# Grouped-query mixer: the value projection issued ahead of the first query projection blocks

## The chip, the cores and the metric

The kernel runs on one core of a Trainium2 chip. The metric is the device time of one execution in microseconds (us); lower is better. Before the change it is 1267.39 us, the median of 3 runs (1267.34 to 1268.09).

## What is computed

A two-layer encoder trunk over 512 tokens of width 1024, in float32. The change lies in the mixer of the second layer, which is grouped-query attention: 16 query heads of 64 share 4 key and value heads.

```python
def odd_mixer(x, mix_norm, w_qkv, q_norm, k_norm, w_out):
    proj = rms_norm(x, mix_norm) @ w_qkv
    q, k, v = jnp.split(proj, [GQA_Q_WIDTH, GQA_Q_WIDTH + GQA_KV_WIDTH], axis=-1)
    q = rms_norm(q.reshape(Bsz, S, GQA_HEADS, GQA_HEAD_DIM), q_norm)
    k = rms_norm(k.reshape(Bsz, S, GQA_KV_HEADS, GQA_HEAD_DIM), k_norm)
    v = v.reshape(Bsz, S, GQA_KV_HEADS, GQA_HEAD_DIM)
    q = apply_rope(q, cos, sin)
    k = apply_rope(k, cos, sin)
    return gqa_block_attention(q, k, v) @ w_out
```

Ahead of it stand the first layer (neighbourhood attention with a state-space scan, then a feed-forward network), behind it a second feed-forward network. Each sub-layer adds its result to `x`.

## The kernel before

Activations lie with the model dimension on the 128 partitions, as 8 tiles of 128 x 512. Every float32 operand is split in a high and a low part (`_h`, `_l`), and a product is three matmuls: high weight by low data, low weight by high data, high by high (`mm3`, lines 162 to 167). A weight block arrives as `_r` by a DMA that SP issues (line 151), ACT rounds it to the high part (line 152), and DVE subtracts to get the low part (line 154). The raw buffer has 2 turns, the high and low ones 3 each.

The mixer's projections are blocks of 24 matmuls of 512 columns (8 tiles of `x` by three): `kpa` and `kpb` for the keys, then for each of 4 head groups g two query blocks `q{g}_0` and `q{g}_1` (`q_blocks`, line 1251). The value projection `gv0` to `gv3` (lines 1375 to 1403) is 4 blocks of 24 matmuls of 256 columns; its weights `wgv` come in two DMAs and are split in four pieces by ACT and DVE, and its result is scaled and split into `gvt0` to `gvt3`. Query and key blocks take turns on 3 PSUM banks, so that a block waits until the block three before it has been read. Score tiles, value blocks and the head norms (`ok_ss`, `oq_ss`, line 1213) share 2 other banks (tag `s`).

When both query blocks of a group are there, `q_finish` (line 1270) makes them ready for the scores: DVE applies the rotary tables (lines 1171 to 1173), PE sums squares over a head (line 1213), DVE and ACT make the reciprocal root (lines 1215, 214 to 216, 208, 209), DVE multiplies (line 1275), ACT and DVE split (lines 1182, 1183; for groups 1 to 3 the split runs on POOL), and SP issues 16 DMAs that stack the parts into `QS{g}_0` to `QS{g}_3` (line 1188). Likewise 16 DMAs stack the keys into `K0` to `K3`.

Attention is a loop of 32 steps i, two per head. A step's `scores` (line 1286) are two tiles `os` of 128 x 512: two matmuls (lines 1293, 1294), a row maximum on DVE (line 1296), an exponential with row sum on ACT (line 1298), a reciprocal on DVE (line 1300), and a scaling on POOL (line 1302). Two steps later `transposes` turns the tiles on PE (line 1311), and ACT and DVE split the turned tile (lines 1314, 1315); three steps later `values` multiplies with `gvt` (lines 1328, 1329) into `oc`.

The source lays the rest of the projections between those steps: a generator `fill` yields after every three matmuls of the query blocks of groups 1, 2, 3 and of the output projection; 8 pieces are drawn ahead of the loop (`OD_FILL`), and then as many per step as `OD_QUOTA` says (5, 5, 4, 2, ...). What is written is a priority and not the final order: for this part of the kernel a list scheduler decides the order on each engine from the dependencies, the buffers and its own estimate of when an operand is ready. The built program's order, shown below, is what each engine follows; it takes its instructions strictly one after another.

Of the kernel before, what the change touches and what calls it, by code (L numbers as in the profile page):

```python
# [77 lines left out]
def encoder_kernel(ctx: ExitStack, tc: tile.TileContext, xt, vec, cst, rope, nab, w_v, w_qk, w_dt, w_ssd,  # L78
                   w_o0, w_t0, w_fa, w_fb, w_kv, w_gv, w_gq, w_o1, out):
    nc = tc.nc  # L80
    V, A, G, T = nc.vector, nc.scalar, nc.gpsimd, nc.tensor
# [13 lines left out]
    def bank(name, tag="p"):  # L95
        if tag in turns:
            turns[tag].append(turns[tag].pop(0))
            tag = turns[tag][-1]
        return pp.tile([P, S], F32, name=name, tag=f"p{tag}", bufs=BANKS[tag])

    def slot(name, dt=F32):
        return sp.tile([P, S], dt, name=name, tag="s")
# [15 lines left out]
    def f(ap):  # L118
        return ap.bitcast(F32)
# [24 lines left out]
    def load_w(src, cols, name, eng=None, los=None):  # L144
        hi = wsp.tile([P, 1024], F32R, name=f"{name}_h", tag="wh", bufs=WH)
        lo = wsp.tile([P, 1024], F32R, name=f"{name}_l", tag="wl", bufs=WL)
        raw = wsp.tile([P, 1024], F32, name=f"{name}_r", tag="wr", bufs=WR)[:, 0:cols]
        parts = src if isinstance(src, list) else [src]
        for n, part in enumerate(parts):
            w = cols // len(parts)  # L150
            nc.sync.dma_start(raw[:, n * w:(n + 1) * w], part)
        A.activation(hi[:, 0:cols], raw, AF.Copy)  # L152
        def low():
            (eng or V).tensor_tensor(lo[:, 0:cols], raw, f(hi)[:, 0:cols], ALU.subtract)  # L154

        if los is None:
            low()
        else:
            los.append(low)
        return hi, lo  # L160

    def mm3(ps, w, wc, x, xc, first, last, wn=P, skip=False):
        (wh, wl), (xh, xl) = w, x
        a, b = slice(wc, wc + wn), xc
        T.matmul(ps, wl[:, a], xh[:, b], start=first, stop=False, skip_group_check=skip)  # L165
        T.matmul(ps, wh[:, a], xl[:, b], start=False, stop=False, skip_group_check=skip)  # L166
        T.matmul(ps, wh[:, a], xh[:, b], start=False, stop=last, skip_group_check=skip)  # L167
# [3 lines left out]
    def stream(blocks, ahead):  # L171
        ws = []
        for n, (_, matmuls) in enumerate(blocks):
            while len(ws) < min(len(blocks), n + 1 + ahead):
                ws.append(blocks[len(ws)][0]())
            yield from matmuls(ws[n])
# [974 lines left out]
    def odd_mixer(op):  # L1151
# [89 lines left out]
        def after(steps, fn):  # L1241
            later.append([steps, fn])

        def step(flush=False):
            for item in list(later):
                item[0] -= 1
                if flush or item[0] <= 0:
                    later.remove(item)
                    item[1]()

        def q_blocks(g, eng):
            banks = []

            def matmuls(w):
                banks.append(bank(f"q{g}_{len(banks)}"))
                for k in range(KB):
                    mm3(banks[-1], w, k * P, xg[k], ALL, k == 0, k == KB - 1)
                    yield
                sq = slot(f"oqsq{g}_{len(banks)}")
                A.activation(sq, banks[-1], AF.Square)  # L1260
                sqs.append(sq)
                if len(sqs) == 2:
                    V.tensor_tensor(sqs[0], sqs[0], sqs[1], ALU.add)
                    after(OD_AFTER, lambda: q_finish(g, banks, sqs[0]))

            sqs = []
            for n in range(2):
                yield (lambda n=n: load_w(w_gq[2 * g + n], 1024, f"wq{g}_{n}", eng)), matmuls

        def q_finish(g, banks, sq):  # L1270
            ra, rb = rotate(*banks, qtab, f"q{g}")
            r = head_rstd(sq, f"oq{g}")
            eng = G if g else V
            for t in (ra, rb):
                V.tensor_tensor(t, t, r, ALU.mult)
            (ah, al), (bh, bl) = split(ra, f"qa{g}", eng=eng), split(rb, f"qb{g}", eng=eng)
            QS = []
            for j in range(4):
                qs = lane(f"QS{g}_{j}", "qs", 7, F32R)
                stack(qs, (ah, bh, al, bl), j)  # L1280
                QS.append(qs)
            qs_of[g] = QS
# [58 lines left out]
        def out_blocks(parts):  # L1341
            per = 8 // (2 * len(parts))

            def matmuls(w, t):
                ps = {}
                for m, part in enumerate(parts):
                    while ctxb[2 * part + 1] is None:
                        yield
                    for n in range(per):
                        o = per * t + n  # L1350
                        if m == 0:
                            ps[o] = bank(f"o1{parts[0]}_{o}")
                        for k in range(2):
                            mm3(ps[o], w, ((m * per + n) * 2 + k) * P, ctxb[2 * part + k], ALL, m + k == 0,
                                k == 1 and part == parts[-1])
                            yield
                        if part == parts[-1]:
                            V.tensor_tensor(res[o], res[o], ps[o], ALU.add)

            def load(t):  # L1360
                half, at = divmod(t * per, 4)
                return load_w([w_o1[part, half][:, 2 * P * at:2 * P * (at + per)] for part in parts], 1024,
                              f"wo{parts[0]}_{t}", V)

            for t in range(8 // per):
                yield (lambda t=t: load(t)), (lambda w, t=t: matmuls(w, t))

        def run(gen, n=None):
            for _ in (gen if n is None else range(n)):
                if n is not None:  # L1370
                    next(gen, None)
                step()

        run(stream(list(q_blocks(0, V)), 1))
        wv = []
        for c in range(4):
            hi, lo = ctxslot(f"wgvh{c}"), ctxslot(f"wgvl{c}")
# [8 lines left out]
        for t in range(4):  # L1386
            ps = bank(f"gv{t}", "s")
            for k in range(KB):
                (wh, wl), (xh, xl) = wv[k // 2], xg[k]
                ts_ = slice(t * P, (t + 1) * P)  # L1390
                ws_ = slice((k % 2) * 256, (k % 2) * 256 + 256)
                T.matmul(ps[:, 0:256], xh[:, ts_], wl[:, ws_], start=k == 0, stop=False)
                T.matmul(ps[:, 0:256], xl[:, ts_], wh[:, ws_], start=False, stop=False)
                T.matmul(ps[:, 0:256], xh[:, ts_], wh[:, ws_], start=False, stop=k == KB - 1)
            vv = slot(f"gvv{t}")
            A.activation(vv[:, 0:256], ps[:, 0:256], AF.Copy, scale=rt[:, t:t + 1])
            v = lane(f"gvt{t}", "vt", 4, F32R)
            vh = v.rearrange("p (h s e) -> p h s e", h=GQ_KV, s=2)
            v4 = vv[:, 0:256].rearrange("p (h e) -> p h e", h=GQ_KV)
            A.activation(vh[:, :, 0], v4, AF.Copy)  # L1400
            V.tensor_tensor(vh[:, :, 1], v4, f(vh[:, :, 0]), ALU.subtract)
            vhl.append(v)
            step(True)
        blocks = (list(q_blocks(1, V)) + list(q_blocks(2, V)) + list(q_blocks(3, V))
                  + [b for parts in ((0, 1), (2, 3)) for b in out_blocks(parts)])
        fill = stream(blocks, 2)
# [24 lines left out]
    with tc.tile_pool(name="op", bufs=1, reuse_waits="tile") as op:  # L1431
        odd_mixer(op)
# [133 lines left out]
```

## Time and profile before

| what | us |
|---|---|
| median of 3 runs | 1267.39 |
| the profiled execution, its own time | 1266.3 |
| span of the profiled execution, first to last instruction | 1264.5 |
| key projection, first matmul | 702.71 |
| first query block, first matmul | 714.39 |
| value projection, first matmul | 727.16 |
| first score matmul | 746.24 |
| PE busy in the span | 1252.1 |
| DVE busy in the span | 991.4 |
| ACT busy in the span | 730.3 |

PE is TensorE's matmul side, PEld its weight loads, DVE VectorE, ACT ScalarE, POOL GpSimd, SP the engine that issues the DMAs. Times are from the start of the span. A matmul's shown duration is longer than the distance to the next one, since matmuls are pipelined; how many fit in a stretch is read from their starts. Of DVE and ACT, too, instructions of one engine overlap by some 0.1 us. In brackets behind a row stands the time that the engine was idle before it, and what ended that.

### The profile page before, as it was taken

To read this page: it belongs to the slowest core of one execution; us is meant where nothing else is said; L and a number is where in the kernel's file an instruction comes from. 1 tells how busy PE (TensorE), PEld (TensorE's weight loads), DVE (VectorE), ACT (ScalarE), POOL (GpSimd) and SP (SyncE) were. 2 spreads that over 40 slices of the span, in tenths; PEclk is the share of its full clock that TensorE was granted. 3 is DMA by queue.
4 is the path that set the end of the run, shared out by engine and by line. 5 is a ranking of instruction groups with operands and counts; after the bars stand their busy time and mean duration, and the time that the engine had idled before them with its cause. 6 is when DMAs were issued, how large, how long until landed. Compare 5 with 4: busy or idle time off the path is not lost.

```text
span 1264.5 us, 20138 instructions
## 1 busy us (share of the span) xinstructions
PE 1252.1 (99%) x7574; PEld 1098.4 (87%) x7574; DVE 991.4 (78%) x1637; ACT 730.3 (58%) x1384; POOL 117.6 (9%) x161
## 2 busy tenths in 40 slices
PE   9999999999999999999999999999999999999998
PEld 8778788888788999989998888788888999889987
DVE  6788798999779988739854879998779988558732
ACT  6676578778464565415643558787554556336521
POOL 5022010011000000000000013444000000000000
PEclk9999999999999999999999999999999999999999
DMA  7335353556243333323223452321242333423132
GB/s 239 109 104 156 112 142 117 166 146 198 79 148 98 104 114 101 117 84 101 78 80 111 133 125 82 95 51 34 71 126 89 116 102 101 117 83 101 55 119 93
DMA packets 54241, 139.03 MB, mean 110 GB/s; under 512 B 7232, under 2 KB 9664, under 8 KB 54144
## 3 DMA queue, kind: packets, MB, share of 16 engines
q1 hardware_dynamic: 53712, 137.13, 35.8%
q8 instruction: 59, 0.97, 0.3%
q10 hardware_dynamic: 432, 0.63, 0.2%
q14 instruction: 38, 0.31, 0.1%
HBM read 127.11 MB, written 2.23 MB: 102 GB/s over the span
## 4 chain that ended last, share of the span: by engine, by line
PE 95%; ACT 2%; DVE 2%; issue 0%; DMA 0%; DVEq 0%; ACTq 0%
PE fo L166 6%; PE fo L167 6%; PE fo L165 6%; PE fa L167 5%; PE fa L166 5%; PE fa L165 5%; PE fu L1029 3%; PE fg L1029 3%; PE g L165 3%; PE g L166 3%; PE g L167 3%; PE fb L167 3%; PE fb L166 3%; PE fb L165 3%; PE opt L1311 2%; PE vps L286 2%
## 5 line engine op out<-in xcount | busy, mean ns | idle before, releaser
L165 PE MATMUL fo<-hh,wf_l 128*128 128x512 f32 x352 | 137.0, 389 | 0.0
L166 PE MATMUL fo<-hl,wf_h 128*128 128x512 f32 x352 | 137.0, 389 | 0.0
L167 PE MATMUL fo<-hh,wf_h 128*128 128x512 f32 x352 | 136.9, 389 | 0.0
L152 ACT ACTIVATE wf_h<-wf_r 128x1024 fp32r<-128x1024 f32 (+1 forms) x72 | 65.5, 913 | 119.2 <-PE fo L167 71.6
L1002 DVE TENSOR_TENSOR xr<-xr,fo 128x512 f32<-128x512 f32 (+1 forms) x49 | 32.1, 673 | 108.8 <-PE fo L167 108.8
L1302 POOL TENSOR_SCALAR op<-op,osum 128x512 f32<-128x512 f32 x64 | 45.6, 726 | 491.2 <-DMA QS<-qa_sh 433.5
L154 DVE TENSOR_TENSOR wf_l<-wf_r,wf_h 128x1024 fp32r<-128x1024 f32 (+1 forms) x72 | 74.0, 1044 | 11.0 <-ACT wf_h L152 11.0
L165 PEld LDWEIGHTS fo<-hh,wf_l 128*128 128x128 f32 x352 | 66.1, 188 | 13.7
L166 PEld LDWEIGHTS fo<-hl,wf_h 128*128 128x128 f32 x352 | 66.1, 188 | 13.7
L167 PEld LDWEIGHTS fo<-hh,wf_h 128*128 128x128 f32 x352 | 66.1, 188 | 13.6
L165 PE MATMUL g<-n_xh,w_l 128*128 128x512 f32 x192 | 76.9, 401 | 0.8 <-ACT grp L546 0.8
L166 PE MATMUL g<-n_xl,w_h 128*128 128x512 f32 x192 | 75.3, 392 | 0.5 <-DVE n_xl L189 0.5
L167 PE MATMUL g<-n_xh,w_h 128*128 128x512 f32 x192 | 75.3, 392 | 0.0
L926 ACT ACTIVATE sl<-sb 128x256 f32<-128x256 f32 x36 | 15.1, 419 | 96.1 <-DVE sb L925 96.1
L1298 ACT ACTIVATE op<-os,omx 128x512 f32<-128x512 f32 x64 | 43.8, 686 | 17.3 <-DVE omx L1296 13.5
L807 ACT ACTIVATE sa<-fa 128x256 f32<-128x256 f32 x72 | 26.9, 374 | 38.1 <-PE fa L167 38.1
L1296 DVE TENSOR_REDUCE omx<-os 128x1 f32<-128x512 f32 x64 | 42.5, 680 | 6.6 <-PE os L1294 6.5
L1315 DVE TENSOR_TENSOR opt<-opt,opt 128x512 fp32r<-128x512 f32 x64 | 43.3, 682 | 4.1 <-ACT opt L1314 3.3
L1314 ACT ACTIVATE opt<-opt 128x512 fp32r<-128x512 f32 x64 | 38.0, 596 | 14.0 <-PE opt L1311 13.3
L810 DVE TENSOR_TENSOR gl<-gr,gh 128x1024 fp32r<-128x1024 f32 x36 | 43.8, 1218 | 0.0
L165 PEld LDWEIGHTS g<-n_xh,w_l 128*128 128x128 f32 x192 | 36.1, 188 | 8.3 <-ACT grp L546 1.2
L807 ACT ACTIVATE gh<-gr 128x1024 fp32r<-128x1024 f32 x36 | 37.7, 1048 | 9.4 <-PE fo L167 9.4
(2745 smaller groups left out, 4305.4 us busy)
## 6 DMA issues: line engine op xcount, KB each, us to landing
ur<-in_w_fa SPq DMA_DIRECT2D x36, 512.0 KB, 3.6
gr<-in_w_fa SPq DMA_DIRECT2D x36, 512.0 KB, 3.6
w_r<-in_w_ssd SPq DMA_DIRECT2D x24, 512.0 KB, 3.6
wf_r<-in_w_fb SPq DMA_DIRECT2D x32, 320.0 KB, 3.0
wf_r<-in_w_fa SPq DMA_DIRECT2D x16, 512.0 KB, 3.6
wf_r<-in_w_fb SPq DMA_DIRECT2D x16, 512.0 KB, 3.5
nb<-in_nab SPq DMA_DIRECT2D x16, 256.0 KB, 3.2
ec<-ecumd SPq DMA_DIRECT2D x32, 128.0 KB, 3.0
```

The lines of the kernel that those rows point to most:

```text
L152: A.activation(hi[:, 0:cols], raw, AF.Copy)
L154: (eng or V).tensor_tensor(lo[:, 0:cols], raw, f(hi)[:, 0:cols], ALU.subtract)
L165: T.matmul(ps, wl[:, a], xh[:, b], start=first, stop=False, skip_group_check=skip)
L166: T.matmul(ps, wh[:, a], xl[:, b], start=False, stop=False, skip_group_check=skip)
L167: T.matmul(ps, wh[:, a], xh[:, b], start=False, stop=last, skip_group_check=skip)
L807: A.activation(dst, src, AF.Copy, scale=scale)
L810: V.tensor_tensor(lo, t, f(hi), ALU.subtract)
L1029: T.matmul(ps, (wl if p == 0 else wh)[:, k * P:k * P + P], xl if p == 1 else xh, start=m == 0, stop=m == 23)
L1296: V.tensor_reduce(mx, sps, AX.X, ALU.max, negate=True)
L1298: A.activation(p_, sps, AF.Exp, bias=mx, accum_out=sums)
L1302: G.tensor_scalar(p_, p_, sums, 1.0, ALU.mult, ALU.mult)
L1315: V.tensor_tensor(hl[:, S:2 * S], pt, f(hl[:, 0:S]), ALU.subtract)
```

## The change

The line that runs the two query blocks of group 0 moves from ahead of the value projection to behind it. Nothing is added or taken away: the same instructions are issued, and each engine has as many as before.

```diff
-        run(stream(list(q_blocks(0, V)), 1))
         wv = []
         for c in range(4):
             hi, lo = ctxslot(f"wgvh{c}"), ctxslot(f"wgvl{c}")
...
             vhl.append(v)
             step(True)
+        run(stream(list(q_blocks(0, V)), 1))
         blocks = (list(q_blocks(1, V)) + list(q_blocks(2, V)) + list(q_blocks(3, V))
                   + [b for parts in ((0, 1), (2, 3)) for b in out_blocks(parts)])
```

The scheduler then gives other orders on PE, DVE, ACT, POOL and SP from the end of the key projection to about the eighteenth attention step; behind that they are the same as before. On PE the value blocks now stand between pieces of `q0_0` and `q0_1`, and the query blocks of groups 1 and 2 follow `q0_1` directly. Three places show it.

PE, the first score tiles (`os_0_7864` and its neighbours are the four tiles of step 0 and 1, `q_1_7889` is `q1_1`), in the order before:

```order
L165 MATMUL q_1_7889<-o_xh,wq_1_l 128x512
L166 MATMUL q_1_7889<-o_xl,wq_1_h 128x512
L1293 MATMUL os_0_7864<-K_7534,QS_0_7695 128x512
L1294 MATMUL os_0_7864<-K_7534,QS_0_7695 128x512
L1293 MATMUL os_1_7871<-K_7534,QS_0_7695 128x512
L1294 MATMUL os_1_7871<-K_7534,QS_0_7695 128x512
L167 MATMUL q_1_7889<-o_xh,wq_1_h 128x512
L165 MATMUL q_1_7889<-o_xh,wq_1_l 128x512
L166 MATMUL q_1_7889<-o_xl,wq_1_h 128x512
```

The same engine from the third score tile on, in the order now (`opt` are the transposes of step 0, `os_0_7949` is the first score tile of head 1):

```order
L167 MATMUL q_0_7941<-o_xh,wq_0_h 128x512
L1293 MATMUL os_2_7906<-K_7534,QS_0_7816 128x512
L1294 MATMUL os_2_7906<-K_7534,QS_0_7816 128x512
L1293 MATMUL os_3_7913<-K_7534,QS_0_7816 128x512
L1294 MATMUL os_3_7913<-K_7534,QS_0_7816 128x512
L1311 MATMUL opt_0_8023<-cstt,op_0_7869 128x128
L1311 MATMUL opt_1_8034<-cstt,op_0_7869 128x128
L1311 MATMUL opt_0_8023<-cstt,op_1_7876 128x128
L1311 MATMUL opt_0_8023<-cstt,op_0_7869 128x128
L1311 MATMUL opt_0_8023<-cstt,op_1_7876 128x128
L1311 MATMUL opt_1_8034<-cstt,op_1_7876 128x128
L1293 MATMUL os_0_7949<-K_7534,QS_1_7821 128x512
```

Before, 29 query matmuls of the groups 1 and 2 stand ahead of the first score matmul, and 55 more between it and the first score tile of step 6 (`os3_0`). Now 66 stand ahead of it, 6 between the second and third score tile, and then none until 13 of `q2_1` shortly before that tile of step 6.

DVE, where the low part of the weights of `q2_1` is made (`wq2_1_l`), in the order before:

```order
L1296 TENSOR_REDUCE omx_7867<-os0_0_7864 128x1
L1296 TENSOR_REDUCE omx_7874<-os0_1_7871 128x1
L154 TENSOR_TENSOR wq2_1_l_7884<-wq2_1_r_7885,wq2_1_h_7883 128x1024
L1300 RECIPROCAL osum_7863<-osum_7863 128x2
L1296 TENSOR_REDUCE omx_7909<-os0_2_7906 128x1
```

And in the order now:

```order
L208 SCALAR_TENSOR_TENSOR oq1_t_7984<-oq1_t_7984,oq1_m_7981 128x512
L1296 TENSOR_REDUCE omx_8098<-os2_0_8095 128x1
L209 SCALAR_TENSOR_TENSOR oq1_r_7983<-oq1_t_7984,oq1_r_7983 128x512
L1300 RECIPROCAL osum_8045<-osum_8045 128x2
L1315 TENSOR_TENSOR opt1_1_8091<-opt1_1_8086,opt1_1_8091 128x512
L1275 TENSOR_TENSOR q1_ra0_7969<-q1_ra0_7969,oq1_r_7983 128x512
L1275 TENSOR_TENSOR q1_ra1_7974<-q1_ra1_7974,oq1_r_7983 128x512
L154 TENSOR_TENSOR wq2_1_l_7884<-wq2_1_r_7885,wq2_1_h_7883 128x1024
L1296 TENSOR_REDUCE omx_8105<-os2_1_8102 128x1
```

It moved from behind the second score tile's maximum to behind the finish of query group 1, with 9 maxima ahead of it in place of 2.

SP, the DMAs that stack keys and queries, and the weight load of `q2_1`, in the order now:

```order
L1188 DMA K_7858<-kab_7528 32x1024
L1188 DMA K_7858<-kab_7529 32x1024
L151 DMA wq_1_r<-in_w_gq 128x1024
L151 DMA wq_0_r<-in_w_gq 128x1024
L1188 DMA QS_0_8000<-qa_sh 32x512
```

Before, that load of `q2_1` stood ahead of all key DMAs; now 14 of the 16 key DMAs, the 16 query DMAs of group 0 and these last two of `K3` come first, and the load of `q3_0` follows.

## The prediction

> **What bounds the kernel now.** I read the page's busy times first, then what PE waits for, then the stretch around the change by windows and by the timeline of each engine.
>
> ```profile
> PE 1252.1 (99%) x7574; PEld 1098.4 (87%) x7574; DVE 991.4 (78%) x1637; ACT 730.3 (58%) x1384; POOL 117.6 (9%) x161
> PE 95%; ACT 2%; DVE 2%; issue 0%; DMA 0%; DVEq 0%; ACTq 0%
> 746.24:771.63 25.39, 25.39 (x138) 21.24 (x137) 21.56 (x39) 17.86 (x41) 9.79 (x12) 1.00 0.46 107
> 771.63:800.00 28.37, 28.34 (x162) 23.73 (x161) 26.95 (x45) 21.92 (x45) 8.58 (x11) 1.00 0.38 115
> 800.00:870.00 70.00, 67.63 (x413) 56.62 (x412) 62.80 (x112) 56.39 (x126) 35.42 (x43) 1.00 0.20 54
> ```
>
> The first two lines are the page's: PE is busy 99% of the span and holds 95% of the chain that ended last. The other three are windows (busy time of PE, PEld, DVE, ACT, POOL): from the first score matmul to the first score tile of step 6, on to 800, and the attention behind that. Early attention loses nothing on PE; later 2.4 us of 70 are idle. So the change can act in two ways only: it takes some of those idle times away, or it brings new ones. The work itself stays.
>
> ```profile
> PE os L1293 <- ACT op L1298: 1.2, 4, 0.6
> PE oq_ss L1213 <- ACT op L1298: 0.5, 1, 0.5
> PE o L165 <- ACT cx_sh L1182: 0.4, 1, 0.4
> ```
>
> These are PE's waits in attention (total, times, longest): 2.1 us. None lies ahead of 780: in the 44 us from 702 to the first score, the part that the change rewrites, PE waits for nothing. There is nothing to win there.
>
> **What moves, on PE.** The orders count 29 query matmuls of groups 1 and 2 ahead of the first score matmul before, and 66 now.
>
> ```profile
> 709.21 4.53 PE kpb L184 x20
> 746.24 0.39 PE L1293 MATMUL os<-K,QS 128*128 128x512 f32 x1
> 771.63 0.48 PE L1293 MATMUL os<-K,QS 128*128 128x512 f32 x1
> 756.15 0.93 PE oq_ss L1213 x2
> 757.07 0.44 PE opt L1311 x4
> 727.16 0.28 PE L1392 MATMUL gv<-wgvl,o_xh 128*128 128x256 f32 x1
> 727.28 0.28 PE L1393 MATMUL gv<-wgvh,o_xl 128*128 128x256 f32 x1
> ```
>
> From the first row (chain), a matmul of 512 columns takes 4.53 / 20 = 0.2265 us of PE. The first score thus comes 37 x 0.2265 = 8.4 us later, at 754.6. Up to the first tile of step 6 PE's work is the same but for one matmul (84 query matmuls then, 85 now), but the fill is spent early: of 55 query matmuls that lay between those two score tiles 19 are left, 13 of them at the end. What matters is whether attention alone, without that fill, keeps PE fed.
>
> **Ahead of the first score.** Value weights now take the first load, query weights the third. The third load needs the buffer of the first, which DVE lets go after the second `wgvl` piece.
>
> ```profile
> 703.43 1.06 ACT L152 ACTIVATE wq_h<-wq_r 128x1024 fp32r<-128x1024 f32 x1 [0.50 <-DMA wq_r<-in_w_gq]
> 707.15 0.74 DVE L189 SCALAR_TENSOR_TENSOR o_xl<-xr,vect,o_xh 128x512 fp32r<-128x512 f32 x1
> 748.10 1.22 DVE L154 TENSOR_TENSOR wq_l<-wq_r,wq_h 128x1024 fp32r<-128x1024 f32 x1
> wq_r<-in_w_gq SPq DMA_DIRECT2D x8, 512.0 KB, 4.2
> ```
>
> The first load lands at 703.4 as before. The second piece stands behind that last `o_xl` and ends near 708.0; the load takes 4.2 us (712.2), ACT 1.06 and DVE 1.22, so `wq0_0_l` is there at 714.6, where PE wants it at 714.4. A wait of some 0.2, and 0.1 more before `gv2`, whose bank the evacuation of `gv0` frees behind ACT's weight rounding: +0.3 us, the first score at 754.9.
>
> **The queries of head 0.** They are now finished behind the value projection, with the 66 query matmuls as cover, 15.0 us and an `oq_ss` of 0.9.
>
> ```profile
> 744.40 0.40 PE L165 MATMUL q<-o_xh,wq_l 128*128 128x512 f32 x1
> 728.30 1.28 DVE L1224 TENSOR_TENSOR kab<-k_ra,kab 128x512 fp32r<-128x512 f32 x2
> 734.57 0.68 DVE L1215 SCALAR_TENSOR_TENSOR oq_m<-oq_ss,oem 128x512 f32<-128x512 f32 x1
> 740.74 0.68 DVE L1183 TENSOR_TENSOR qb_sl<-q_ra,qb_sh 128x512 fp32r<-128x512 f32 x1
> 741.99 0.54 SPq L1188 DMA_DIRECT2D QS<-qb_sl  x1
> QS<-qa_sh SPq DMA_DIRECT2D x8, 64.0 KB, 2.0
> 750.17 6.18 SPq L1188 DMA_DIRECT2D K<-kab  x9
> ```
>
> At 744.40 the blocks of group 0, the values, 21 matmuls of `q1_0` (4.8 us) and an `oq_ss` (0.9) are done before; without the last two and with the 0.3, `q0_1` ends at 739.0 now. Behind it ACT squares (0.6), and DVE has the sum of squares, three rotary steps and a weight split (1.1 us) before `oq_m`: near 744.1. From `oq_m` to the end of `qb_sl` it is 741.42 - 734.57 = 6.9 us, then the fourth DMA is issued (0.6) and lands (2.0): 753.6. PE arrives at 754.9: no wait, with 1.3 us to spare. The 14 key DMAs ahead of these on SP take 6.18 / 9 = 0.69 each, 9.7 us; even from 729.6, where DVE splits the keys before, they are issued by 739.3.
>
> **Attention without fill.** This is the term that decides. The chain of one step, before:
>
> ```profile
> 746.89 1.29 DVE L1296 TENSOR_REDUCE omx<-os 128x1 f32<-128x512 f32 x2 [0.91 <-PE os L1294]
> 747.62 0.69 ACT L1298 ACTIVATE op<-os,omx 128x512 f32<-128x512 f32 x1 [0.66 <-DVE omx L1296]
> 748.30 0.68 ACT L1298 ACTIVATE op<-os,omx 128x512 f32<-128x512 f32 x1
> 749.55 1.37 POOL L1302 TENSOR_SCALAR op<-op,osum 128x512 f32<-128x512 f32 x2 [433.51 <-DMA QS<-qa_sh]
> 752.63 1.82 POOL L1302 TENSOR_SCALAR op<-op,osum 128x512 f32<-128x512 f32 x2 [1.72 <-PE q L167]
> ```
>
> From the first score matmul (746.24) to the scaled tiles (750.92) it is 4.7 us. I lay these durations along the new orders, with zero at the first score matmul. PE has two tiles and six query matmuls, to 2.27; the third tile to 2.72; the fourth waits for the second exponential's bank, to 3.25. Then stand the transposes, whose tiles POOL gives at 3.9 and 4.6: PE waits 1.3 in all. Small waits of 0.3 follow up to 10.0, where `os2_0` needs the bank of `os1_2`. Its maximum stands on DVE behind two splits and three steps of query group 1 and ends at 10.8, the exponential at 11.6: 1.6. `os2_2` needs the exponential of `os2_0`, behind another step of group 1 on DVE: 0.9. The first matmul of `q2_1`, which could fill, needs `wq2_1_l`, now behind all that: 1.4 more. The waits walked one by one make 5.5 us; DVE's list gives the same from its side.
>
> ```profile
> L1296 DVE TENSOR_REDUCE omx<-os 128x1 f32<-128x512 f32 x12 | 7.8, 681 | 1.6 <-PE os L1294 1.6
> L1315 DVE TENSOR_TENSOR opt<-opt,opt 128x512 fp32r<-128x512 f32 x7 | 4.7, 678 | 0.5 <-ACT opt L1314 0.4
> L1275 DVE TENSOR_TENSOR q_ra<-q_ra,oq_r 128x512 f32<-128x512 f32 x2 | 1.3, 685 | 0.0
> L1300 DVE RECIPROCAL osum<-osum 128x2 f32<-128x2 f32 x6 | 1.0, 161 | 1.9 <-ACT op L1298 1.9
> ```
>
> DVE's list up to it: 9 maxima, 4 transposed tiles, 7 steps of group 1, each 0.61 (1.29 for two in a row is 0.61 and an end of 0.68), 4 reciprocals of 0.1, the weight split of 1.2: 12.2 + 0.4 + 1.2 = 13.8 us. To that come DVE's own idle times in the start: 0.65 for the first score, 0.9 for the row sums, 1.45 until the first transposes let PE go on, 0.2 later. The sum is 17.0. PE's work ahead of `q2_1` is 22 + 6 matmuls of 0.2265, one `oq_ss` of 0.93, 24 transposes of 0.11 and 16 value matmuls of 0.12 (from the two `gv` rows): 6.3 + 0.9 + 2.6 + 1.9 = 11.8. So PE waits 17.0 - 11.8 = 5.2 us in this stretch, which I take, since it has fewer roundings. Behind it PE has 1.8 us of `q2_1` in a row and DVE's backlog is no larger than before (`wq3_0_l` is already done), so I add nothing.
>
> **Sum.** Ahead of the first score +0.3; attention without fill +5.2; less about 0.2, by which the window of 25.39 us before is longer than its work (79 x 0.2265 + 0.93 + 32 x 0.11 + 24 x 0.12 = 25.2). +5.3 us: the span goes from 1264.5 to 1269.8, the execution from its own 1266.3 to 1271.6, and the median, 1.1 above that execution, from 1267.39 to 1272.7.
>
> **Bounds.** Below: the 3.0 us of idle in DVE's start are the least certain, since they rest on a chain that the trace shows only under fill. If half of it is hidden, 1.5 less. Above: POOL's pair takes 1.82 in one row in place of 1.37; if that meets each of three steps that PE waits for, 1.4 more. The 2.1 us of later waits may go, or come twice, as POOL and ACT orders differ up to step 18: 2.1 each way, taken in part. The trace shows no attention without fill, so neither end is measured. One price decides nothing alone: the load of `q2_1` is now behind 18 stacking DMAs; the first of them near 749.6 (5.6 behind `oq_m`, as before), 18 x 0.69 = 12.4 and 4.2 for the load end at 766.2, 11.3 after the first score, and ACT asks for it near 14.5.
>
> **A rule beside it.** The Trainium skill, "Perfetto Trace Analysis", "Optimization Strategy", says that where the most-contended engine changes over time, interleaving the regimes may help. The windows agree: with fill, PE is busy 25.39 of 25.39 us and DVE 21.56; the order now sets a stretch of DVE work apart. The page gives no figure.
>
> **The rivals.**
>
> Later waits go and early ones don't come (faster). In the order now DVE has five steps of query group 1 done before the first maximum, 5 x 0.61 = 3 us that stood between maxima before. If that lead lets the maxima come in time, PE doesn't wait early, and the 2.1 us of later waits, all on ACT behind DVE, go as well: 1267.4 - 2.1 = 1265.3. It decides from the point at which DVE's list up to `wq2_1_l` is under 11.8 us with its idle; I count 17.0. 5%.
>
> PE takes the wait back (no change). PEld, the weight loads, is busy 21.24 of 25.39 us in the stretch; if PE could run at that pace behind a wait, the 4.1 us left there and the like behind it would cover 5.2, and the time stays at 1267.4 to 1268. Against it: the row of 20 matmuls has one each 0.2265 us with nothing to wait for, and no row of this shape goes faster. The Trainium skill ("Perfetto Trace Analysis", "Identifying the Most-Contended Engine") judges TensorE by weight-load share and not by matmul share, which by 87% would call it not full. The 0.2265 us say that it is. 10%.
>
> The score waits for its queries as well (slower still). The 1.3 us to spare go if the weight split or the row sums come late on DVE, or the DMA lands at 4 us as some key DMAs would: +2 us, 1274.7. It is 13%.
>
> **How the numbers follow.** The forecast has 72%, at 1272.7 us, by itself 1270.4 (the hidden half, and 0.8 of the later waits) to 1275 (POOL's 1.4 and 0.9 of them). The range takes in the late queries and part of the smaller waits: 1269.4 to 1276. A measurement can tell about 0.2%, 2.5 us, so slower begins at 1269.9: the forecast and the late queries, 85%. Within 0.2% is the wait taken back, 10%; faster 5%.
>
> **What would show it.** In the profile after: the first score matmul near 754.9 (span time), PE's waits in the 18 us behind it at about 5 us in place of 0, named `opt` on POOL, `os` on ACT, `q` on DVE `wq_l`; the first tile of step 6 near 777; the rest shifted by the same 5 us with its waits near 2 us. It is wrong if PE shows under 2.5 us there, if the first score is before 753 or after 756.5, or if the shift at step 6 isn't there at the end.

## The result, and the profile after

The changed kernel takes 1276.05 us, the median of 4 runs (1275.07 to 1277.03), beside 1267.47 us for the kernel before in 4 runs: 8.6 us more, a ratio of 1.0067 with a 95% interval of 1.0049 to 1.0084. Slower was forecast, by 5.3 us; the time lies 0.05 us above the top of the range.

The profiled execution after takes 1276.0 us, its span is 1274.2. The first fence has two lines of its page (busy times, and the engines' shares of the chain that ended last), the second PE's timeline (start, duration) at the first matmul of the key projection, the first score tile, the first tile of step 6 and the first matmul of the feed-forward network behind the mixer.

```profile
PE 1255.2 (99%) x7574; PEld 1098.6 (86%) x7574; DVE 992.0 (78%) x1637; ACT 730.8 (57%) x1384; POOL 120.3 (9%) x161
PE 92%; ACT 3%; DVE 3%; issue 1%; DMA 1%; POOL 0%; SPq 0%; DVEq 0%; ACTq 0%; POOLq 0%
```

```profile
703.95 0.39 PE L184 MATMUL kpa<-o_xh,wka_l 128*128 128x512 f32 x1
755.93 0.39 PE L1293 MATMUL os<-K,QS 128*128 128x512 f32 x1
780.01 0.39 PE L1293 MATMUL os<-K,QS 128*128 128x512 f32 x1
925.07 0.39 PE L1029 MATMUL fg<-f_xh,wf_l 128*128 128x512 f32 x1
```

The same last mark in the kernel before, and then windows, before (from the first score tile to the feed-forward) and after (to step 6, and to the feed-forward); their columns are window, length, and busy times of PE, PEld, DVE, ACT and POOL.

```profile
915.33 0.39 PE L1029 MATMUL fg<-f_xh,wf_l 128*128 128x512 f32 x1
```

```profile
746.24:915.33 169.09, 166.69 (x955) 139.57 (x954) 147.43 (x251) 124.31 (x261) 62.02 (x77) 1.00 0.26 72
```

```profile
755.93:780.01 24.08, 19.15 (x102) 14.27 (x101) 20.44 (x34) 17.64 (x39) 12.18 (x12) 1.00 0.35 93
755.93:925.07 169.14, 160.41 (x918) 132.30 (x917) 145.05 (x246) 124.00 (x260) 65.55 (x77) 1.00 0.25 70
```

The mixer takes 212.62 us before (915.33 - 702.71) and 221.12 now: 8.50 more. The rest of the 9.7 between the spans lies ahead of the mixer, 703.95 against 702.71, where no instruction is changed; the profiled execution of before was quicker there, as its 1266.3 beside a median of 1267.39 says.

Inside the mixer the first score comes 8.45 us later (51.98 us behind `kpa` in place of 43.53), as 37 query matmuls of 0.2265 us do. And then attention takes 169.14 us as it took 169.09, though 37 matmuls fewer stand in it. Nothing that was done ahead was given back: the whole 8.4 us are lost. PE's waits after, from the first score tile to the first of step 6 and (second fence) from there to the feed-forward network (total, times, longest):

```profile
PE os L1293 <- ACT op L1298: 1.8, 2, 1.2
PE q L165 <- DVE wq_l L154: 1.7, 1, 1.7
PE oq_ss L1213 <- ACT op L1298: 0.9, 1, 0.9
PE opt L1311 <- POOL op L1302: 0.5, 2, 0.3
```

```profile
PE os L1293 <- ACT op L1298: 1.9, 4, 0.8
PE oq_ss L1213 <- ACT op L1298: 1.3, 1, 1.3
PE oc L1328 <- DVE opt L1315: 0.2, 1, 0.2
```

4.9 us stand in the first stretch, where none stood before, and 3.4 behind it in place of 2.1. The names are the forecast ones, and `oq_ss`, which the forecast had not waiting early. PE loses more than the named waits show: up to step 6 its stretch is 6.8 us longer than its work (the section on the experiments says how this is reckoned), and behind step 6 it loses 1.6 us more than before.

### The profile page after: what moved, and what is told of

Read it like the earlier page. It is cut to its first block, busy times and chain, and to the rows that moved or that the text cites. A ratio compares the mean times of both kernels' runs of the same rounds, so it can differ in the third digit from the quotient of the medians.

```text
span 1274.2 us, 20132 instructions
## 1 busy us (share of the span) xinstructions
PE 1255.2 (99%) x7574; PEld 1098.6 (86%) x7574; DVE 992.0 (78%) x1637; ACT 730.8 (57%) x1384; POOL 120.3 (9%) x161
## 4 chain that ended last, share of the span: by engine, by line
PE 92%; ACT 3%; DVE 3%; issue 1%; DMA 1%; POOL 0%; SPq 0%; DVEq 0%; ACTq 0%; POOLq 0%
PE fo L166 6%; PE fo L167 6%; PE fo L165 6%; PE fa L167 5%; PE fa L166 5%; PE fa L165 5%; PE fu L1029 3%; PE fg L1029 3%; PE g L165 3%; PE g L166 3%; PE g L167 3%; PE fb L167 3%; PE fb L166 3%; PE fb L165 3%; PE vps L286 2%; PE opt L1311 1%
## 5 line engine op out<-in xcount | busy, mean ns | idle before, releaser
L1298 ACT ACTIVATE op<-os,omx 128x512 f32<-128x512 f32 x64 | 43.7, 687 | 16.9 <-DVE omx L1296 14.2
```

The source lines that it names most:

```text
L1298: A.activation(p_, sps, AF.Exp, bias=mx, accum_out=sums)
```

## The experiments

The theories. **A**: what costs is the number of query matmuls spent ahead of attention, which are then missing as fill between its steps. **B**: the place of the value blocks or the order of the weight loads costs. **C**: single late things cost, the weights of `q2_1` or the norm's score bank. **D**: DVE and POOL, which slow each other. **E** and **F** ask what attention without fill is bound by: DVE's list (E), or the latency of the chain through all engines (F).

The table gives for each kernel the query matmuls of groups 1 to 3 ahead of the first score tile and from there to step 6 (counted in the orders), what PE loses up to step 6 and from there to the feed-forward network, how much longer the mixer is than before's 212.62 us, and the median above that of the kernel before run beside it (1267.47, 1267.06 or 1267.36 us). What PE loses is the stretch's length less that of the same work in the kernel before. That is 25.39 us up to step 6, where the kernel before did not wait, and 143.70 behind it, which holds that kernel's own late waits. For each piece of PE's work that stands in another stretch than before, this is set right by the prediction's rows: 0.2265 us for a query matmul, 0.93 for the two `oq_ss` of a group, 0.11 for a transpose and 0.12 for a value matmul. So in early_fill_only 23 query matmuls, the `oq_ss` of group 1, 4 transposes and 4 value matmuls fewer stand in the first stretch, whose work is 18.3 us. Mixer and medians agree within 0.6 us, save for 1.0 in before_no_max.

| kernel | ahead | to step 6 | lost to step 6 | lost behind it | mixer | median above before |
|---|---|---|---|---|---|---|
| changed kernel | 66 | 19 | 6.8 | 1.6 | +8.5 | +8.6 |
| early_fill_only | 66 | 32 | 1.8 | 1.5 | +3.3 | +3.3 |
| loads_first | 65 | 19 | 7.1 | 0.9 | +8.1 | +8.7 |
| behind_one | 33 | 39 | 2.1 | 1.4 | +3.4 | +3.2 |
| behind_two | 52 | 32 | 5.3 | 0.9 | +6.0 | +6.1 |
| early_q21 | 73 | 36 | 3.0 | 6.6 | +9.6 | +9.7 |
| norm_bank_t | 62 | 22 | 5.9 | 1.5 | +7.4 | +7.2 |
| split_on_dve | 66 | 25 | 6.7 | 0.2 | +7.0 | +6.4 |
| early_q21_bank | 69 | 39 | 1.4 | 4.6 | +6.4 | +6.8 |
| before_no_max | 29 | 55 | -0.1 | -4.6 | -4.6 | -5.6 |
| after_no_max | 66 | 6 | 3.8 | -2.8 | +1.0 | +0.7 |
| before_split_dve | 29 | 55 | 0.3 | 0.3 | +0.6 | +0.3 |
| after_split_bank | 62 | 24 | 6.6 | 3.4 | +10.1 | +10.1 |

The 95% intervals of the ratios reach 0.1 to 0.2% to each side, 1.1 to 2.2 us. Where two changed versions differ by 1 to 3 us, the intervals overlap or nearly touch, and the reading rests on one trace of each. A loss below zero means less time there than in the kernel before.

**early_fill_only**, the kernel before with the fill spent early:

```diff
-OD_FILL = 8
+OD_FILL = 22
-OD_QUOTA = (5, 5, 4, 2, ...
+OD_QUOTA = (0, 0, 0, 2, ...
```

> The kernel before with the value projection in its old place, but with 66 query matmuls of groups 1 and 2 ahead of the first score tile, as many as in the changed kernel. Theory A (spent fill: attention's own chain over DVE, ACT and POOL takes about 24.1 us from the first score tile to the first of step 6, the changed kernel's own time there, and every query matmul of 0.2265 us missing below about 50 shows as PE idle): 32 query matmuls are left in that stretch, work 17.1 + 13 x 0.2265 = 20.0 us, so PE waits about 4 us there, and 0 to 1.3 behind it: 1271.4 to 1272.8. Theory B (the place of the value blocks or of their weight loads is what costs): no more than before, 1266.5 to 1268.5. Theory C (late weights of q2_1 and the norm's score bank are what costs, not the number): q2_1 runs early here, so at most 1 us, 1268.4.

1270.34 us (ratio 1.0028, 1.0017 to 1.0039). Spending the fill costs 3.3 us without any move of the value blocks, so B is not all of it. A's sum is too high: it took the stretch to last 24.1 us, and it lasts 20.15. PE loses 1.8 us there, where A had 4, and 1.5 behind step 6, where A had up to 1.3. The first score comes 52.78 us behind `kpa`, 0.8 later than in the changed kernel, but that is no loss: the `oq_ss` of group 1 stands ahead of it here. That row, and PE's only named wait up to step 6:

```profile
753.68 1.02 PE L1213 MATMUL oq_ss<-oqsq,cstt 128*128 128x512 f32 x2
...
PE opt L1311 <- POOL op L1302: 0.8, 1, 0.8
```

With the same 66 matmuls ahead the changed kernel loses 5.3 us more, so the number spent ahead does not alone set the cost.

**loads_first**, the changed kernel with the loads in their old order:

```diff
         wv = []
+        qb0 = list(q_blocks(0, V))
+        ws0 = [load() for load, _ in qb0]
...
-        run(stream(list(q_blocks(0, V)), 1))
+        for w0, (_, matmuls0) in zip(ws0, qb0):
+            run(matmuls0(w0))
```

> The changed kernel with the two weight blocks of query group 0 loaded ahead of the value weights, as before the change; 65 query matmuls stand ahead of the first score tile. Theory A: 19 to 20 query matmuls are left up to step 6, as in the changed kernel: 1274.5 to 1276.5, PE waits near 7 us in the stretch. Theory B (order of the weight loads): the cost goes, 1267.5 to 1270. Theory C: as A, since the weights of q2_1 stay late.

1275.75 us (1.0068, 1.0055 to 1.0081), as the changed kernel: the order of the loads costs nothing that shows.

**behind_one** and **behind_two** put the query blocks behind the first and the second value block (here one, the other with `t == 2`):

```diff
         for t in range(4):
+            if t == 1:
+                run(stream(list(q_blocks(0, V)), 1))
...
-        run(stream(list(q_blocks(0, V)), 1))
```

> The changed kernel with the query blocks of group 0 written behind the first value block in place of behind the fourth; 33 query matmuls ahead of the first score tile, and 39 from there to the first tile of step 6, none of them between os2_0 and os3_0. Theory A by its sum: work 17.1 + 20 x 0.2265 = 21.6 us against a chain of 24.1, 2.5 us of PE waits, all of them behind os2_0: 1269.5 to 1271. Theory B: the loads of the value weights still come first, so the cost of the changed kernel stays, 1274 to 1277. Theory C: q2_1 comes late here too, so 1.7 to 2.6 us of waits, 1269.1 to 1270; the trace has to part it from A, by whether PE waits for wq_l or for os and opt.

> The changed kernel with the query blocks of group 0 written behind the second value block; 52 query matmuls ahead of the first score tile, 32 from there to the first tile of step 6. Theory A: work 20.0 us against 24.1, PE waits of 4.1, 1271.4 to 1272.8, between behind_one and the changed kernel. Theory B: as the changed kernel, 1274 to 1277. Theory C: q2_1 as late as in behind_one, so the same time as behind_one within 0.7 us.

1270.3 us (1.0025, 1.0016 to 1.0035) and 1273.17 (1.0044, 1.0032 to 1.0057): inside A's range, and 0.4 above it. With 33, 52 and 66 matmuls ahead the cost is 3.2, 6.1 and 8.6. B falls as to the loads with behind_one, which still loads the value weights first, and C with the 2.9 us between the two, where it allowed 0.7. In behind_one PE waits at `os` and `opt` (0.9 and 0.6 us) and not for `wq_l`. PE's waits of behind_two up to step 6 are others than the changed kernel's:

```profile
PE opt L1311 <- DVE opt L1315: 1.9, 1, 1.9
PE os L1293 <- ACT op L1298: 0.4, 1, 0.4
```

No `wq_l` is in them, though `q2_1` starts late here too. Its stretch was run at a granted clock of 0.93 (the third last column), so of the 5.3 us lost in it up to 25.43 x 0.07 = 1.8 are clock:

```profile
752.26:777.69 25.43, 22.95 (x116) 17.77 (x114) 22.39 (x39) 18.12 (x40) 12.39 (x14) 0.93 0.42 109
```

**early_q21** has the weights of `q2_1` early:

```diff
+        w21 = blocks[3][0]()
+        blocks[3] = ((lambda: w21), blocks[3][1])
         fill = stream(blocks, 2)
```

> The changed kernel, with the weights of q2_1 loaded ahead of the other fill's, so that they are split long before attention begins and q2_1 can stand between the first steps. It spends even more ahead of the first score tile: 73 query matmuls (66 in the changed kernel), and 36 stand between there and the first tile of step 6, in pieces of 3 to 14. Theory A in its strict form (the number spent ahead sets the cost; so far 29: 0, 33: 3.2, 52: 6.1, 66: 8.6 us above the kernel before): 1275.5 to 1278. Theory C (what costs is that no query matmul is free when a score tile has to wait, since q2_1's weights come late and the rest is spent): the stretch from the first score tile to step 6 loses under 1.5 us, as where the early fill alone was spent and q2_1 was early, with its late 2 to 3 us behind: 1269.5 to 1272.

1276.8 us (1.0075, 1.0063 to 1.0088), inside the range of A's strict form; C falls as to the late weights, by the time and by the 3.0 us that PE loses up to step 6. That is 3.8 less than in the changed kernel, but behind step 6 it loses 5.0 more. Of these up to 1.7 are clock: for 3.4 us the granted clock was 0.50 in this execution (second fence, a window). Its longest waits behind step 6:

```profile
PE o L166 <- POOL cx_sl L1183: 1.9, 1, 1.9
PE os L1293 <- ACT op L1298: 1.3, 4, 0.6
PE oq_ss L1213 <- ACT op L1298: 1.2, 1, 1.2
PE oc L1328 <- DVE ocx L1337: 0.9, 2, 0.7
```

```profile
813.60:817.00 3.40, 3.17 (x13) 2.36 (x12) 3.14 (x6) 1.27 (x3) 1.36 (x2) 0.50 0.48 109
```

What fills a gap early is missing later, now down to the output projection `o`: its first matmul comes at 807.87 in place of 812.63, and it then waits for POOL.

**norm_bank_t** and **split_on_dve** take away one wait each, **early_q21_bank** joins the first of them to early_q21:

```diff
-            ps = bank(f"{name}_ss", "s")
+            ps = bank(f"{name}_ss", "t")
```

```diff
-            eng = G if g else V
+            eng = G if g > 1 else V
```

> The changed kernel with the sums of squares of the head norms written to the transposes' banks in place of the score banks, so that a norm's matmul no longer waits for an exponential to free a score bank; 62 query matmuls ahead of the first score tile, 22 up to step 6, q2_1 still late. Theory C by the bank (the two waits of oq_ss, 0.9 and 1.3 us, and the restart of PE behind each): 1273.3 to 1275. Theory A or C by the late weights of q2_1: the wait only moves to the next score tile, 1275 to 1277.

> The changed kernel with the weight split of query group 1 (two subtractions) on DVE in place of POOL; 66 query matmuls ahead of the first score tile. Theory D (POOL and DVE slow each other while both run: 2.31 us for POOL's pair of scalings in place of 1.36, DVE's split of q2_1's weights 1.62 and 1.71 in place of 1.22, and this is what made the stretch longer than forecast): 1 to 2 us less than the changed kernel, 1274 to 1275. Against it (DVE's list bounds the stretch, and two subtractions of 0.68 more lengthen it): 1276.5 to 1278.

> The weights of q2_1 early and the norms' sums in the transposes' banks, together: 69 query matmuls ahead of the first score tile, 40 up to step 6. Theory C: the two causes add, 1268 to 1271, near the kernel before. Theory A in its strict form: 1274.5 to 1277.

1274.21 us (1.0059, 1.0045 to 1.0072), 1273.46 (1.0054, 1.0042 to 1.0067) and 1273.88 (1.0052, 1.0039 to 1.0065). Against the kernel before run beside it, the bank gives 1.4 of the 8.6 back and the split 2.2 (by the bare medians 1.8 and 2.6). The bank's time lies inside C's range for that wait. The split's lies below both of its ranges, and the gain does not come by D's way: up to step 6 PE's waits are those of the changed kernel to the tenth, and it lies behind, where PE loses 0.2 us in place of 1.6 and `oq_ss` waits 0.5 in place of 1.3. What DVE's slower steps cost by themselves the run does not part off, since DVE has two subtractions of 0.68 us more in it. In split_on_dve, up to step 6 and, below the dots, behind it:

```profile
PE os L1293 <- ACT op L1298: 1.8, 2, 1.2
PE q L165 <- DVE wq_l L154: 1.7, 1, 1.7
PE oq_ss L1213 <- ACT op L1298: 0.9, 1, 0.9
PE opt L1311 <- POOL op L1302: 0.5, 2, 0.3
...
PE oq_ss L1213 <- ACT op L1298: 0.5, 1, 0.5
```

early_q21_bank (39 matmuls up to step 6, not the 40 of its expectation) lies between the two ranges expected and decides nothing.

**before_no_max** and **after_no_max** take the maxima out of both kernels:

```diff
-                V.tensor_reduce(mx, sps, AX.X, ALU.max, negate=True)
...
-                A.activation(p_, sps, AF.Exp, bias=mx, accum_out=sums)
+                A.activation(p_, sps, AF.Exp, scale=0.0625, accum_out=sums)
```

> The kernel before with the row maxima of all score tiles left out (64 DVE instructions of about 0.61 us, 39 us; the exponential is taken of 0.0625 times the score instead, so its values are others). 29 query matmuls ahead of the first score tile. It is the partner of the next run. PE's work is unchanged and PE is the bound in the kernel before, so only its later waits of 2.1 us can go: 1264.5 to 1267.

> The changed kernel with the same left out; 66 query matmuls ahead of the first score tile, 6 from there to the first tile of step 6. Theory E (attention can't go faster than DVE's list in it, so query matmuls taken out of it leave PE idle, wherever the rest stands): with 39 us off DVE, PE's waits go down to what ACT's exponentials and splits leave, 1 to 3 us, so the time is 1 to 3.5 above the run before_no_max, 1265.5 to 1270. Theory F (the latency of the chain score, exponential, scaling, transpose, whatever DVE's load): the maximum is one link of five in it (0.9 of 4.7 us), so most of the cost stays, 5 to 7 above before_no_max. Theory B (place of the value blocks or loads): 8 to 9 above it.

1261.72 us (0.9959, 0.9947 to 0.9972) and 1268.03 (1.0008, 0.9999 to 1.0017): 6.3 apart (5.5 by the mixers), where the kernels with maxima are 8.6 apart. E falls, F's 5 to 7 holds. Up to step 6 after_no_max has DVE busy for half the time only, and PE still waits for exponentials (the window's busy times in the order given above):

```profile
754.97:771.69 16.72, 14.58 (x77) 10.39 (x75) 8.51 (x18) 12.31 (x33) 7.58 (x10) 1.00 0.41 114
```

```profile
PE os L1293 <- ACT op L1297: 1.9, 3, 0.8
```

So without the 39 us of maxima the cost is 2.3 us less, about a quarter; the rest is there without them. How much of the 2.3 is DVE's time is open, since the order changed as well: 6 query matmuls stand up to step 6 in place of 19. before_no_max is quicker than expected, which the last section takes up.

**before_split_dve** and **after_split_bank** try whether a better version comes out:

> The kernel before with the weight split of query group 1 on DVE in place of POOL, the edit that took 2.6 us off the changed kernel, to see whether it is a gain of its own. If it took away waits that only the changed kernel has: no difference, 1266.3 to 1267.8. If the two subtractions were too late on POOL in both kernels (2.25 us each there, 0.68 on DVE): 1265 to 1266.3.

> The changed kernel with both edits that helped it, group 1's split on DVE and the norms' sums in the transposes' banks; 62 query matmuls ahead of the first score tile, 24 up to the first tile of step 6. If the two gains (2.6 and 1.9 us) are of different waits and add: 1270.5 to 1272.5. If both took the same late waits: 1272.5 to 1274.

1267.65 us (1.0003, 0.9994 to 1.0012): no gain in the kernel before. 1277.45 (1.0084, 1.0071 to 1.0096), above both ranges: the two edits that helped singly gain nothing together. It is 1.4 us slower than the changed kernel, though the two intervals overlap. Its order is another again, and 1.7 us of waits for turned tiles (norm_bank_t has them too) and 1.5 for POOL's `cx_sl` are not in the changed kernel (below the dots, behind step 6):

```profile
PE oc L1328 <- DVE opt L1315: 1.7, 3, 0.6
PE q L165 <- DVE wq_l L154: 1.2, 1, 1.2
...
PE o L166 <- POOL cx_sl L1183: 1.5, 2, 1.1
```

No version here with the full computation beats the kernel before.

**What stays open.** The same 66 matmuls spent early cost 3.3 us with the value blocks in their old place and 8.6 in the new one. Part of that is how many query matmuls are left between the first score and step 6. With the maxima in, PE loses nothing there with 55 left, 2.1 and 1.4 us with 39, 3.0 with 36, 5.3 (up to 1.8 of it clock) with 32, and 5.9 to 7.1 with 25 or fewer. Only early_fill_only, 1.8 with 32, lies well below that series. The traces suggest why: with the value blocks in their old place group 0 is finished early, and group 1's finish then runs under the fill that is spent ahead. These are group 1's products, ended by the reciprocal root, in the kernel before, in early_fill_only and in the changed kernel:

```profile
763.17 1.28 DVE L1275 TENSOR_TENSOR q_ra<-q_ra,oq_r 128x512 f32<-128x512 f32 x2
```

```profile
755.92 0.39 PE L1293 MATMUL os<-K,QS 128*128 128x512 f32 x1
...
760.89 1.28 DVE L1275 TENSOR_TENSOR q_ra<-q_ra,oq_r 128x512 f32<-128x512 f32 x2
```

```profile
771.25 1.49 DVE L1275 TENSOR_TENSOR q_ra<-q_ra,oq_r 128x512 f32<-128x512 f32 x2
```

They come 16.9, 5.0 and 15.3 us behind the first score tile. Before, DVE had them late but PE had 55 matmuls of fill; in early_fill_only there is less fill but DVE is done early; the changed kernel has neither. behind_two, with 14.5 us and 32 matmuls, fits by what it loses up to step 6. What is lost behind step 6, most of all the 6.6 us of early_q21 (15.3 us, 36 matmuls), this does not account for. It is argued from a few traces; no run moved this one thing alone.

## Why the prediction was right, and where it was too small

**Right: the lag of the first score.** 37 x 0.2265 = 8.4 us was forecast and 8.45 measured between `kpa` and the first score. The 0.3 us ahead of it did not show (0.07). The score did not wait for its queries, so that rival (13%) falls, as the 1.3 us to spare said: in the trace the fourth DMA lands at 754.47, 1.46 us ahead of the score.

**Right: attention without fill, by its cause.** The waits came where they were laid, under the names given: `opt` on POOL, `os` on ACT, `q` on DVE's `wq_l`. That they add up to 4.9 us, near the 5.2, is partly luck: `opt` waits 0.5 where 1.3 was laid, `os` 1.8 for 2.5, `wq_l` 1.7 for 1.4, and `oq_ss` 0.9 for nothing. Of the signs that were named, the shift of 5 us did not stay at that: it is 8.5 at the end of the mixer. Neither of the other rivals came: no wait was taken back at PEld's pace (10%), and the later waits did not go (5%). The Trainium skill's rule that was weighed ("Perfetto Trace Analysis", "Optimization Strategy": interleave regimes with different limits) agrees with early_fill_only, where spending the fill ahead by itself cost 3.3 us.

**Too small: DVE's list, 17.0 us forecast, 18.4 measured.** This is the term of 5.2. `q2_1` started 18.41 us behind the first score (774.34 - 755.93), and DVE's list up to there holds rows that were longer than forecast (the last row is ACT's):

```profile
758.79 0.17 DVE L1300 RECIPROCAL osum<-osum 128x2 f32<-128x2 f32 x1 [0.92 <-ACT op L1298]
761.69 0.69 DVE L1296 TENSOR_REDUCE omx<-os 128x1 f32<-128x512 f32 x1 [1.42 <-PE os L1294]
765.43 0.89 DVE L1173 TENSOR_TENSOR q_ra<-q_ra,q_rb 128x512 f32<-128x512 f32 x1
768.77 0.69 DVE L208 SCALAR_TENSOR_TENSOR oq_t<-oq_t,oq_m 128x512 f32<-128x512 f32 x1 [0.65 <-ACT oq_t L216]
772.66 1.62 DVE L154 TENSOR_TENSOR wq_l<-wq_r,wq_h 128x1024 fp32r<-128x1024 f32 x1
771.32 1.05 ACT L152 ACTIVATE wq_h<-wq_r 128x1024 fp32r<-128x1024 f32 x1
```

DVE's idle times came as estimated, 0.92 and 1.42 for 0.9 and 1.45; one was 0.65 for 0.2. Another 0.8 are steps that ran beside POOL: 0.89 in place of 0.68, the products 1.49 in place of 1.28, the weight split 1.62 in place of 1.22. The bounds had POOL slower beside DVE, not DVE beside POOL, though the trace of before has a step of 0.90 us beside POOL as well (`q_ra`, line 1173, at 758.05). One wait was overlooked: `oq_ss` takes a score bank too, so it waits 0.9 for an exponential. With 0.4 more behind the start of `q2_1`, step 6 came at 24.08 us in place of 22.2 (25.39 - 36 x 0.2265 + 5.2 - 0.2).

DVE's list dates the start of `q2_1`, but it is not its only cause. ACT finished rounding the same weights at 772.37, 0.3 us before DVE began their split, so a shorter list of DVE would have gained no more than that while ACT kept its times. In after_no_max, with DVE idle half the time, the same split starts at 772.62, 17.65 us behind the first score (here 16.73). That the list came as near as it did is in part luck, then.

**Wrong: nothing added behind step 6.** "DVE's backlog is no larger than before" was the step. From step 6 to the feed-forward network it is 145.06 us in place of 143.70, with one query matmul fewer behind it: 1.6 us more. Of the named waits there, `oq_ss` grew from 0.5 to 1.3 and `os` from 1.2 to 1.9. Together: 0.2 less ahead, 1.8 more in the stretch, 1.6 more behind, 3.2 of the 3.3 by which the forecast fell short. early_q21 loses 6.6 us behind step 6, early_q21_bank 4.6: there too, what is saved early is lost later.

## What to carry to other kernels

Work that moves ahead on the bounding engine is no gain if it was the cover of a later stretch: compare that stretch's length before and after, less the moved work. Ask what covers the latency of each finish step, and what will cover it once the cover is moved; here the scheduler paid with the only fill that attention had. Closing one wait with the remaining fill opened another in most of these runs, and two edits that helped singly gained nothing together, so such edits are to be measured together.

## What the runs showed of the hardware

**A wait of PE costs more than its name says.** PE's timeline of the changed kernel at two waits:

```profile
772.04 0.60 PE L1311 MATMUL opt<-cstt,op 128*128 128x128 f32 x4
774.34 0.50 PE L165 MATMUL q<-o_xh,wq_l 128*128 128x512 f32 x1 [1.71 <-DVE wq_l L154]
774.68 0.39 PE L166 MATMUL q<-o_xl,wq_h 128*128 128x512 f32 x1
...
779.34 0.60 PE L1311 MATMUL opt<-cstt,op 128*128 128x128 f32 x4
779.70 0.48 PE L165 MATMUL q<-o_xh,wq_l 128*128 128x512 f32 x1
780.01 0.39 PE L1293 MATMUL os<-K,QS 128*128 128x512 f32 x1
```

From four transposes to the second matmul behind them it takes 0.67 us without a wait (780.01 - 779.34) and 2.64 with one (774.68 - 772.04): 1.97 more, of which 1.71 is named. So 0.26 us is lost at this wait beside the named time, and counts as busy. Six waits of `os` behind transposes in the changed kernel, set beside sequences of the same matmuls without a wait, lose 0.27 to 0.28 each in the same way. At 0.26 each, the six waits up to step 6 make 1.6 of the 1.9 us between the 6.8 that PE loses there and the 4.9 named; this is an estimate. It is also part of why before_no_max gained 5.6 us where 2.1 were named: behind step 6 it has PE busy for 138.90 us, beside 141.31 in the kernel before, for the same matmuls. Of these 2.4 us the six late waits of the kernel before make 1.6 by the same estimate; the rest is open.

```profile
772.87:912.01 139.14, 138.90 (x820) 119.03 (x818) 96.28 (x160) 101.07 (x221) 57.36 (x63) 1.00 0.23 67
```

```profile
771.63:915.33 143.70, 141.31 (x820) 118.33 (x819) 125.87 (x213) 106.45 (x221) 52.23 (x65) 1.00 0.23 66
```

**DVE and POOL lengthen each other.** POOL's timeline in the changed kernel, and (second fence) the same subtraction over the kernel before (shortest, median and longest duration in ns):

```profile
764.43 1.36 POOL L1302 TENSOR_SCALAR op<-op,osum 128x512 f32<-128x512 f32 x2 [0.42 <-DVE osum L1300]
770.91 2.31 POOL L1302 TENSOR_SCALAR op<-op,osum 128x512 f32<-128x512 f32 x2 [5.12 <-DVE osum L1300]
773.19 2.25 POOL L1183 TENSOR_TENSOR qa_sl<-q_ra,qa_sh 128x512 fp32r<-128x512 f32 x1
```

```profile
L1183 POOL TENSOR_TENSOR qa_sl<-q_ra,qa_sh x3: 1279/1291/1292, 764.7 to 828.0; 128x512 fp32r<-128x512 f32 x3
```

Beside DVE's products and weight split POOL's pair takes 2.31 us in place of 1.36 and the subtraction 2.25 in place of 1.29, while the DVE rows above grow too. It is not always both: at 765.43 DVE's step takes 0.89, but POOL's pair beside it (764.43) keeps its 1.36. The Trainium skill, "SBUF — State Buffer", "SBUF: two separate sides", says that an instruction of DVE with two operands in SBUF and one of POOL that reads SBUF exclude each other for a whole instruction. The slowed DVE rows are of that kind, so the trace agrees as far as it goes; who held the port when, it does not show. split_on_dve bears it out with one number: without POOL's subtraction beside it, the second weight split takes 1.21 us (in the changed kernel 1.71).

```profile
773.51 1.21 DVE L154 TENSOR_TENSOR wq_l<-wq_r,wq_h 128x1024 fp32r<-128x1024 f32 x1
```
